# Weight loads moved to another queue, and a residual read back in quarters, in the down-projection of a hybrid decoder layer

## The chip, the cores and the metric

The kernel runs on one core of a Trainium2 chip. A core has five engines that run side by side, each through its own list of instructions in a fixed order: TensorE (PE in the profile: the matmuls, and PEld: the weight loads into its array), VectorE (DVE), ScalarE (ACT), GpSimd (POOL) and SyncE (SP). Transfers between the main memory (HBM) and the on-chip memory are issued by SP, ACT or POOL and carried out by 16 shared DMA engines; an instruction that issues a transfer first waits for what it needs, and everything behind it on that engine waits with it. The metric is device time in microseconds (us) for one launch.

## The reference, cut to what matters

One trunk layer for 512 tokens of width 1024. An attention sub-layer gives a residual stream x; then follows a gated MLP whose down-projection is the place of the change:

```python
def conv_ffn(h, w_up, conv_w, conv_b, w_down):
    u = h @ w_up                       # 1024 -> 2 * 2816
    up = jnp.pad(u, ((0, 0), (CONV_WIDTH - 1, 0), (0, 0)))
    c = conv_b + conv_w[0] * up[:, 0:s]
    for j in range(1, CONV_WIDTH):
        c = c + conv_w[j] * up[:, j:j + s]
    val, gate = jnp.split(c, 2, axis=-1)
    return (jax.nn.silu(gate) * val) @ w_down      # 2816 -> 1024
...
        h2 = rmsnorm(x, ffn_norm_g[l])
        x = x + conv_ffn(h2, w_up[l], conv_w[l], conv_b[l], w_down[l]).astype(x.dtype)
```

All values are float32.

## The kernel before, in words

Float32 products are made from pairs of a high and a low part: ACT copies a weight tile `raw` to its rounded high part `whi`, DVE subtracts to get the low part `wlo` (`wsplit_`, L288 to L306), and PE multiplies high by high, low by high and high by low. `raw` has three buffers, `whi` and `wlo` two each. `wload` (L271) issues the next load of the list `weight_tiles` from SP. A load must wait until the `wlo` of the tile three places earlier has been made, since that read the same buffer; a `whi` must wait until PE has read the one two places earlier.

The up-projection (L1385 to L1402) makes 22 blocks of 128 features. In each, the convolution is built in `cgq` by ACT and DVE, and the result is split into parts for the down-projection. Before it, the residual `x1` (2 MB) was written to main memory as `x1d` (L1354); its room is used otherwise.

The down-projection (L1475 to L1574) uses a scheme with seven products in place of eight for a two by two partition: the 2816 weight rows come in 11 pairs of 128 rows (g = 0 to 10), the tokens in two halves, the columns in two halves. One product of a pair, both token tiles of a half, is six matmuls (four with `whi`, two with `wlo`). It runs in four stretches; inside them the order on every engine is that of the code:

- **The first pass** (L1481 to L1493) uses six pieces of weights, here called A0 to A5: A0 holds one pair, the others two pairs each.
- **The second pass** (L1494 to L1508) uses six more, B0 to B5, in the same way.
- **The loop over pairs** (L1511 to L1542) makes four products per pair from sums of the four weight blocks of the pair. DVE makes these sums in place in the raw tiles: `sum_13` (two additions; the first reads only the first 128 rows of the pair, the second both), then `sum_24` (two more). `sum_hi` lets ACT copy the high parts, `sum_lo` lets DVE make the low parts.
- **The last pass** (L1545 to L1574) uses the pieces for the seventh product, while the results are added to the residual (`add_to`, in part on POOL) and stored.

The raw tiles of the odd pairs come through `wload`. Those of the even pairs go to `sraw` (two tiles of 512 KB), which lies in the room of `cgq`: `sum_load` (L1432 to L1440) issues them from SP, so for pair 0 SP waits there until the last convolution no longer needs `cgq`. `sum_load(0)` stands ahead of the whole first pass (L1478), `sum_load(2)` in its last step, the others in the loop. For pair 0, `sum_13` runs in step 3 of the first pass, `sum_24` and `sum_hi` in step 4, `sum_lo` in step 5. In step i of a pass, `produce` splits piece i+1 and loads piece i+3 of the same list.

The residual is read back into `x1b` by one POOL transfer (L1406), as soon as the room of the up-projection's input is free; its first use is `add_to(0, 0, P2)` in the second pass (L1499), the next POOL's addition at the start of the loop (L1525), the rest after the loop.

Of the kernel before, what the change touches and what calls it, by code (L numbers as in the profile page):

```python
# [21 lines left out]
NT = S // 128  # L22
# [60 lines left out]
def hybrid_block(ctx: ExitStack, tc: tile.TileContext, A: dict, out: bass.AP):  # L83
    nc = tc.nc
# [24 lines left out]
    def bank(tag, bufs, shape=(128, 512)):  # L109
        return ps.tile(list(shape), F32, name="ps_" + tag, tag=tag, bufs=bufs)  # L110

    def mmb():
        return bank("mm", 4)

    def pa():
        return bank("a", 2)
# [154 lines left out]
    def wload():  # L271
        nxt = next(wtiles, None)
        if nxt is not None:
            src, kt, n, eng = nxt
            raw = wp.tile([128, kt, n], F32, name="raw", tag="raw", bufs=3)
            nc.sync.dma_start(raw, src if len(src.shape) == 3 else src.rearrange("(k p) n -> p k n", p=128))
            loads.append((raw, kt, n, eng))
# [997 lines left out]
    x1 = xr.tile([128, NT, D], F32, name="x1", tag="x1")  # L1275
# [39 lines left out]
    with tc.manual_schedule(engines=KTS):  # L1315
        for t in range(NT):
            qs = slice(128 * t, 128 * t + 128)
            p = mmb()
# [34 lines left out]
    x1d = dp.tile([128, NT * D], F32, name="x1d")  # L1353
# [31 lines left out]
    for f in range(NF):  # L1385
# [4 lines left out]
        g = f // 2  # L1390
# [12 lines left out]


    x1 = xr.tile([128, NT, D], F32, name="x1b", tag="hh2")
    nc.gpsimd.dma_start(x1.rearrange("p t d -> p (t d)"), x1d)  # L1406
    ring = xr.tile([128, 2, 2, 2, 512], F32R, name="ring", tag="hl2")
    sraw = cgq[:, 0:8].rearrange("p (r a) n -> p r (a n)", r=2)

    def product(banks, x, w, first=False, end=False, ts_=(0, 1)):  # L1410

        for n, (x_, y) in enumerate(((x[0], w[0]), (x[1], w[0]), (x[0], w[1]))):
            for t in ts_:
                mm(banks[t], x_[:, 128 * t:128 * t + 128], y, first and n == 0, end and n == 2)

    def res(t, c, n=512, c0=0):
        return x1[:, t, 512 * c + c0:512 * c + c0 + n]

    def add_to(half, c, src, op=ALU.add, eng=None):
        for i in range(2):  # L1420
            o = res(2 * half + i, c)
            (eng or v).tensor_tensor(o, o, src[i], op=op)  # L1422

    def store(half, c):
        for t in (2 * half, 2 * half + 1):
            nc.gpsimd.dma_start(out[0][128 * t:128 * t + 128, 512 * c:512 * c + 512], res(t, c))  # L1426
# [3 lines left out]
    raws = {}  # L1430

    def sum_load(g):  # L1432
        if g >= NG:
            return
        if g % 2:
            raws[g] = [loads.pop(0)[0][:, 0] for _ in range(2)]
        else:
            raws[g] = [sraw[:, i] for i in range(2)]
            for i in range(2):
                nc.sync.dma_start(raws[g][i], A["w_down"][0][256 * g + 128 * i:256 * g + 128 * i + 128])  # L1440

    def sum_13(g):
        if g < NG:
            b1, b2 = raws[g]
            tt(b1[:, 0:512], b1[:, 0:512], b1[:, 512:1024], ALU.add)
            tt(b1[:, 512:1024], b1[:, 512:1024], b2[:, 512:1024], ALU.add)

    def sum_24(g):
        if g < NG:
            b1, b2 = raws[g]  # L1450
            tt(b2[:, 512:1024], b2[:, 512:1024], b1[:, 0:512], ALU.add)
            tt(b2[:, 0:512], b2[:, 0:512], b2[:, 512:1024], ALU.add)

    def sum_hi(g, i):
        if g % 2:
            hi = wp.tile([128, 2, 512], F32R, name="whi", tag="whi", bufs=2)
            lo = wp.tile([128, 2, 512], F32R, name="wlo", tag="wlo", bufs=2)
        else:
            hi, lo = ring[:, i, 0], ring[:, i, 1]
        act(hi, raws[g][i].rearrange("p (b n) -> p b n", b=2))  # L1460
        return hi, lo

    def sum_lo(g, i, hi, lo):
        tt(lo, raws[g][i].rearrange("p (b n) -> p b n", b=2), hi.bitcast(F32), ALU.subtract)
        return [(hi[:, b], lo[:, b]) for b in range(2)]

    def produce():
        wsplit()
        wload()
# [6 lines left out]
    with tc.manual_schedule(engines=everything):  # L1476
        wload()
        sum_load(0)  # L1478
        P2, P1 = [mmb(), mmb()], [pa(), pa()]
        T = {}  # L1480
        for i, gs in enumerate(DOWN):  # L1481
            w = ahead.pop(0)
            produce()
            if i == 3:
                sum_13(0)
            elif i == 4:
                sum_24(0)
                h = [sum_hi(0, 0), sum_hi(0, 1)]
            elif i == 5:
                T[0] = [sum_lo(0, k, *h[k]) for k in range(2)]  # L1490
                sum_load(2)
            for j, g in enumerate(gs):
                product(P2, (a2[:, 0, g, 0], a2[:, 1, g, 0]), [x[:, j] for x in w], g == 0, g == NG - 1)  # L1493
        for i, gs in enumerate(DOWN):  # L1494
            w = ahead.pop(0)
            if i < len(DOWN) - 1:
                produce()
            if i == 1:
                add_to(0, 0, P2)  # L1499
            elif i == 2:  # L1500
                two_parts(a2[:, 0, 0:6, 0], a2[:, 1, 0:6, 0], ql[:, 0:6])
            elif i == 3:
                two_parts(a2[:, 0, 6:NG, 0], a2[:, 1, 6:NG, 0], ql[:, 6:NG])
            elif i == 5:
                sum_load(1)
                sum_13(1)
            for j, g in enumerate(gs):
                product(P1, (a1[:, 0, g], a1[:, 1, g]), [x[:, j] for x in w], g == 0, g == NG - 1)  # L1508
        u = [[ql[:, 4 * k + 2 * t:4 * k + 2 * t + 2].rearrange("p a n -> p (a n)") for t in range(2)] for k in range(2)]
        P4, P5, P7 = [mmb(), mmb()], [mmb(), mmb()], [pb(), pb()]  # L1510
        for g in range(NG):  # L1511
            n, last = g + 1, g == NG - 1
            if not last:
                h13 = sum_hi(n, 0)
                sum_24(n)
                h24 = sum_hi(n, 1)
                T[n] = [sum_lo(n, 0, *h13), sum_lo(n, 1, *h24)]
                if n % 2:
                    wload()
                    wload()  # L1520
                sum_load(n + 2)
                if g == 0:
                    act_copy(u[0], P1)
                    P6 = [pa(), pa()]
                    add_to(0, 0, u[0], eng=nc.gpsimd)  # L1525
                    store(0, 0)
                if g in (2, 4, 6):
                    k = g // 2 - 1
                    two_parts(a1[:, 0, k], a1[:, 1, k], q4[k])
                if g == NG - 2:  # L1530
                    two_parts(a1[:, 0, 3:5], a1[:, 1, 3:5], ql[:, 14:16])
                    two_parts(a1[:, 0, 5:7], a1[:, 1, 5:7], cgq[:, 8:10])
                sum_13(g + 2)
            else:
                produce()
                produce()
                two_parts(a1[:, 0, 7:NG], a1[:, 1, 7:NG], cgq[:, 10:14])
            (t1, t3), (t4, t2) = T.pop(g)
            product(P5, split[D1][g], t1, g == 0, last)
            product(P7, split[D3][g], t3, g == 0, last)  # L1540
            product(P4, (a2[:, 0, g, 1], a2[:, 1, g, 1]), t4, g == 0, last)
            product(P6, split[N2][g], t2, g == 0, last)  # L1542
        add_to(1, 0, P7)
        add_to(1, 1, P7, ALU.subtract)
        P3 = [pb(), pb()]  # L1545
        for i, gs in enumerate(DOWN[:-2]):
            w = ahead.pop(0)
            for j, g in enumerate(gs):
                product(P3, split[Q4][g], [x[:, j] for x in w], g == 0)
            produce()  # L1550
            if i == 0:
                add_to(1, 0, P4)
            elif i == 1:
                for t in range(2):
                    tt(u[0][t], u[0][t], P6[t], ALU.add)
                add_to(1, 0, u[0], eng=nc.gpsimd)
                store(1, 0)
            elif i == 2:
                for t in range(2):
                    tt(u[1][t], u[0][t], P5[t], ALU.add)  # L1560
                for h_ in (1, 0):
                    add_to(h_, 1, u[1], ALU.subtract, nc.gpsimd)
                    if h_:
                        store(1, 1)
        ends = [(gs, ahead.pop(0)) for gs in DOWN[-2:]]
        for t in range(2):
            for gs, w in ends:
                for j, g in enumerate(gs):
                    product(P3, split[Q4][g], [x[:, j] for x in w], False, g == NG - 1, ts_=(t,))
            n = 256 if t else 512  # L1570
            for c0 in range(0, 512, n):
                o = res(t, 1, n, c0)
                tt(o, o, P3[t][:, c0:c0 + n], ALU.subtract)
                (sc if c0 else nc.sync).dma_start(out[0][128 * t:128 * t + 128, 512 + c0:512 + c0 + n], o)  # L1574
# [28 lines left out]
```

## Time and profile before

| | |
|---|---|
| time, median of 3 runs | 854.68 us (854.37 to 855.96) |
| the profiled execution | 856.35 us, of which 854.2 us are the span that the profile shows |
| transfers issued by SP, whole run | 80.59 MB, 32.3% of the 16 DMA engines' time |
| transfers issued by POOL, whole run | 7.62 MB, 2.7% |

The profile is of one execution, on the same clock throughout, in microseconds from the start of the span. A row of its time order gives start, length, engine, line of the code, operation and, in brackets, how long the engine had been idle and what released it. A line can be that of a helper: L122 is every matmul, L125 every ACT copy, L276 every `wload`, L305 every `wlo` of a piece, L128 the other DVE additions and subtractions, L1440 the loads of `sum_load`. The view by stretches gives, for a stretch of time, the busy time of each engine with the number of its instructions, and then the TensorE clock that was granted (1.00 is full speed) and the share of the DMA engines in use.

### The profile page before, as it was taken

The page shows a single profiled execution, that of the slowest core. Times are in us where ns is not written, and L with a number is a line of the kernel's source. Part 1 is how long each engine was busy: PE and PEld are TensorE (multiplying, and loading weights), DVE is VectorE, ACT ScalarE, POOL GpSimd, SP SyncE. Part 2 cuts the span into 40 slices and gives each one's busy share as a digit, 9 for nine tenths or more (in the row PEclk, how much of TensorE's full clock was granted, in tenths as well). Part 3 has the DMA queues.
Part 4 walks back from the last instruction along what each step waited for, and adds up shares of the span by engine and source line. Part 5 has one row for each costly group of instructions (what it writes and reads, how often), then busy time and mean ns, then how long its engine had stood idle before and what let it go on. Part 6 is the DMA issues. An engine that isn't in the chain of part 4 may idle for free.

```text
span 854.2 us, 13060 instructions
## 1 busy us (share of the span) xinstructions
PE 823.0 (96%) x5039; PEld 669.3 (78%) x5039; DVE 603.0 (71%) x1150; ACT 440.1 (52%) x845; POOL 68.9 (8%) x85
## 2 busy tenths in 40 slices
PE   7999999999999999999999999999999999689996
PEld 5877878887777886777788888888888888468885
DVE  4578779963555678888675666666667666569984
ACT  6776654552545677767343454444444444344441
POOL 5200010040000010111000000000000000002005
PEclk9999999999999999999999999999999999799999
DMA  7513222335462330010166233333333332755652
GB/s 217 133 50 79 82 75 75 77 106 165 124 123 51 79 72 13 17 35 26 51 231 201 99 98 93 93 95 93 97 99 99 98 99 62 258 194 176 196 160 99
DMA packets 110706, 91.59 MB, mean 107 GB/s; under 512 B 4189, under 2 KB 98068, under 8 KB 110388
## 3 DMA queue, kind: packets, MB, share of 16 engines
q1 hardware_dynamic: 107344, 80.59, 32.3%
q0 software_dynamic: 2240, 7.62, 2.7%
q10 hardware_dynamic: 1060, 2.55, 1.0%
q8 instruction: 39, 0.64, 0.3%
q14 instruction: 23, 0.19, 0.1%
HBM read 85.30 MB, written 4.39 MB: 105 GB/s over the span
## 4 chain that ended last, share of the span: by engine, by line
PE 48%; DMA 2%; DVE 1%; POOL 1%; ACT 0%; issue 0%; SPq 0%; POOLq 0%; DVEq 0%; ACTq 0%
PE ps_mm L122 42%; PE ps_a L122 3%; PE ps_b L122 3%; DMA raw<-in_w_down_dram 2%; POOL x1b L1422 1%; DVE hl L137 0%; DVE wlo L305 0%; ACT whi L125 0%; POOL out_dram L1426 0%; PE ps_b L1211 0%; PE ps_a L202 0%; PE ps_mm L1211 0%; DVE cgq L137 0%; DVE cgq L128 0%; ACT hh L125 0%
## 5 line engine op out<-in xcount | busy, mean ns | idle before, releaser
L122 PE MATMUL ps_mm<-hh,whi 128*128 128x512 f32 (+1 forms) x624 | 242.8, 391 | 0.4 <-ACT hh L125 0.3
L122 PE MATMUL ps_mm<-hl,whi 128*128 128x512 f32 (+1 forms) x624 | 239.0, 385 | 0.3 <-DVE hl L137 0.2
L305 DVE TENSOR_TENSOR wlo<-raw,whi 128x1024 fp32r<-128x1024 f32 (+1 forms) x107 | 125.1, 1170 | 110.2 <-PE ps_mm L122 71.4
L125 ACT ACTIVATE whi<-raw 128x1024 fp32r<-128x1024 f32 (+2 forms) x130 | 128.5, 989 | 124.4 <-PE ps_mm L122 55.9
L122 PE MATMUL ps_mm<-hh,wlo 128*128 128x512 f32 (+1 forms) x624 | 152.7, 384 | 0.0
L122 PEld LDWEIGHTS ps_mm<-hh,whi 128*128 128x128 f32 x624 | 117.2, 188 | 26.3 <-ACT hh L125 0.8
L122 PEld LDWEIGHTS ps_mm<-hl,whi 128*128 128x128 f32 x624 | 117.3, 188 | 23.3 <-DVE hl L137 1.0
L122 PEld LDWEIGHTS ps_mm<-hh,wlo 128*128 128x128 f32 x624 | 115.1, 188 | 23.3
L137 DVE SCALAR_TENSOR_TENSOR cgq<-ps_mm,cw,cgq 128x511 f32<-128x511 f32 (+1 forms) x88 | 65.4, 746 | 1.6
L125 ACT ACTIVATE cgq<-ps_mm,cw 128x512 f32<-128x512 f32 x44 | 34.4, 781 | 19.3 <-PE ps_mm L122 18.7
L125 ACT ACTIVATE P<-P,nm 128x512 f32<-128x512 f32 (+3 forms) x64 | 35.4, 553 | 14.9 <-DVE nm L1185 14.9
L125 ACT ACTIVATE a<-cgq 128x512 fp32r<-128x512 f32 (+2 forms) x24 | 13.2, 550 | 56.6 <-DVE cgq L128 56.6
L128 DVE TENSOR_TENSOR cgq<-cgq 128x512 f32<-128x512 f32 (+1 forms) x52 | 36.4, 700 | 1.7 <-ACT cgq L125 0.3
L125 ACT ACTIVATE cgq<-cgq 128x512 f32<-128x512 f32 x22 | 13.9, 633 | 45.2 <-DVE cgq L137 45.2
L1185 DVE CUSTOM_DVE_ANT_0 P<-ps_a,AB 128x512 f32<-128x512 f32 (+3 forms) x64 | 29.3, 482 | 4.2 <-PE ps_a L122 3.7
L305 POOL TENSOR_TENSOR wlo<-raw,whi 128x512 fp32r<-128x512 f32 (+3 forms) x13 | 20.4, 1570 | 136.0 <-PE ps_mm L122 57.3
L122 PE MATMUL ps_mm<-whi,a 128*128 128x512 f32 x64 | 19.0, 422 | 8.2 <-ACT whi L125 8.2
L122 PE MATMUL ps_a<-KH,qst 128*128 128x512 f32 (+3 forms) x64 | 21.3, 348 | 1.5 <-DVE nm L1185 0.9
L122 PE MATMUL ps_mm<-whi,hh 128*128 128x280 f32 (+2 forms) x72 | 22.6, 333 | 0.2 <-DVE AB L128 0.2
L125 ACT ACTIVATE QK<-ps_mm 128x64 f32<-128x64 f32 (+5 forms) x56 | 14.9, 308 | 14.4 <-PE ps_mm L122 14.3
L125 ACT ACTIVATE ring<-cgq 128x1024 fp32r<-128x1024 f32 x12 | 12.7, 1061 | 18.5 <-DVE cgq L128 14.7
L122 PEld LDWEIGHTS ps_mm<-whi,a 128*128 128x128 f32 x64 | 13.0, 205 | 11.4 <-ACT whi L125 8.6
(425 smaller groups left out, 1489.5 us busy)
## 6 DMA issues: line engine op xcount, KB each, us to landing
raw<-in_w_up_dram SPq DMA_DIRECT2D x44, 512.0 KB, 3.8
raw<-in_w_in_dram SPq DMA_DIRECT2D x38, 512.0 KB, 4.0
raw<-in_w_down_dram SPq DMA_DIRECT2D x25, 512.0 KB, 4.2
cgq<-in_w_down_dram SPq DMA_DIRECT2D x12, 512.0 KB, 3.7
raw<-in_w_out_dram SPq DMA_DIRECT2D x8, 512.0 KB, 3.6
xt<-in_x_dram SPq DMA_DIRECT2D x4, 512.0 KB, 5.8
raw<-in_cmp_w_k_dram SPq DMA_DIRECT2D x4, 512.0 KB, 3.8
raw<-in_cmp_w_v_dram SPq DMA_DIRECT2D x4, 512.0 KB, 4.5
```

What stands on the lines that cost most here:

```text
L122: te.matmul(o, lhsT=l, rhs=r, start=start, stop=stop)
L125: sc.activation(o, i, f, **kw)
L128: v.tensor_tensor(o, a, b, op=op)
L137: v.scalar_tensor_tensor(o, a, s, b, op0=op0, op1=op1)
L305: eng.tensor_tensor(lo, raw, hi.bitcast(F32), op=ALU.subtract)
L1185: v.tensor_tensor_reduce(out=P[:, i], in0=sp[:, N * (i - i0):N * (i - i0) + N], in1=BT[:, h, 384 - 128 * qt:512], scale=-1.0, scalar=-NEG, ...
L1422: (eng or v).tensor_tensor(o, o, src[i], op=op)
```

## The change

The loads of `sum_load` are issued by POOL's queue and no longer by SP's. The single read-back of the residual becomes four of 512 KB (two token tiles by 512 columns), each issued where the code now says `reload`: the first ahead of the first pass, right behind `sum_load(0)`, the others in the loop at g = 3, 5 and 7, right behind a `sum_load`.

```diff
     x1 = xr.tile([128, NT, D], F32, name="x1b", tag="hh2")
-    nc.gpsimd.dma_start(x1.rearrange("p t d -> p (t d)"), x1d)
...
+    def reload(half, c):
+        h_ = slice(2 * half, 2 * half + 2)
+        nc.gpsimd.dma_start(x1[:, h_, 512 * c:512 * c + 512],
+                            x1d.rearrange("p (t d) -> p t d", t=NT)[:, h_, 512 * c:512 * c + 512])
...
             for i in range(2):
-                nc.sync.dma_start(raws[g][i], A["w_down"][0][256 * g + 128 * i:256 * g + 128 * i + 128])
+                nc.gpsimd.dma_start(raws[g][i], A["w_down"][0][256 * g + 128 * i:256 * g + 128 * i + 128])
...
         wload()
         sum_load(0)
+        reload(0, 0)
...
                     store(0, 0)
+                if g in (3, 5, 7):
+                    reload(*((1, 0), (1, 1), (0, 1))[g // 2 - 1])
```

On SP, from the first load of the down-projection on, the order before is this (128x512 is a piece of one pair, 128x2x512 of two, `cgq` the loads of an even pair, 128x1024 those of an odd one):

```order
L276 DMA raw<-in_w_down_dram 128x512
L276 DMA raw<-in_w_down_dram 128x2x512 x2
L1440 DMA cgq<-in_w_down_dram 128x1024 x2
L276 DMA raw<-in_w_down_dram 128x2x512 x3
L276 DMA raw<-in_w_down_dram 128x512
L276 DMA raw<-in_w_down_dram 128x2x512 x2
L1440 DMA cgq<-in_w_down_dram 128x1024 x2
L276 DMA raw<-in_w_down_dram 128x2x512 x3
```

With the change the same stretch of SP's list, and a little beyond, is this:

```order
L276 DMA raw<-in_w_down_dram 128x512
L276 DMA raw<-in_w_down_dram 128x2x512 x5
L276 DMA raw<-in_w_down_dram 128x512
L276 DMA raw<-in_w_down_dram 128x2x512 x5
L276 DMA raw<-in_w_down_dram 128x1024 x10
```

So A3 to A5 stand directly behind A0 to A2, and B3 to B5 directly behind B0 to B2, with nothing of the even pairs between them. Those loads are now on POOL, whose list with the change reads so, from the start of the down-projection to the first addition after the loop (L1444 is the load of `sum_load`, L1425 a `reload`, L1421 POOL's `add_to`, L1430 a store):

```order
L1444 DMA cgq<-in_w_down_dram 128x1024 x2
L1425 DMA x1b<-x1d 128x2x512
L1444 DMA cgq<-in_w_down_dram 128x1024 x2
L1421 TENSOR_TENSOR x1b<-x1b,ql 128x512 x2
L1430 DMA out_dram<-x1b 128x512 x2
L1444 DMA cgq<-in_w_down_dram 128x1024 x4
L1425 DMA x1b<-x1d 128x2x512
L1444 DMA cgq<-in_w_down_dram 128x1024 x2
L1425 DMA x1b<-x1d 128x2x512
L1444 DMA cgq<-in_w_down_dram 128x1024 x2
L1425 DMA x1b<-x1d 128x2x512
L1421 TENSOR_TENSOR x1b<-x1b,ql 128x512 x2
```

Before, POOL had only the one read-back ahead of the first two additions here; now two loads and a quarter stand ahead of the next two loads, and the three other quarters lie between the loads of the loop. The last convolution belongs to a part whose order a scheduler chooses, and there DVE's list moves too, at the seam between the up-projection and the first pass (- before, + with the change; `a_5128` and `d_5129` are parts of the activations, `cgq<-ql,cgq` is the last use of the convolution's room, the `cgq` row with x2 is `sum_13` of pair 0):

```order
 L128 TENSOR_TENSOR cgq<-cgq 128x512
 L128 TENSOR_TENSOR cgq<-cgq 128x256
-L137 SCALAR_TENSOR_TENSOR ql<-cgq 128x256
+L305 TENSOR_TENSOR wlo<-raw,whi 128x1024
 L128 TENSOR_TENSOR a_5128<-cgq,a_5128 128x512
 L128 TENSOR_TENSOR d_5129<-cgq,d_5129 128x256
+L137 SCALAR_TENSOR_TENSOR ql<-cgq 128x256
 L137 SCALAR_TENSOR_TENSOR cgq<-ql,cgq 128x256
-L305 TENSOR_TENSOR wlo<-raw,whi 128x1024 x2
+L305 TENSOR_TENSOR wlo<-raw,whi 128x1024
 L128 TENSOR_TENSOR cgq<-cgq 128x512 x2
 L305 TENSOR_TENSOR wlo<-raw,whi 128x1024
```

The `wlo` of A3 has moved ahead of the last four small operations of the convolution, and with it the last use of `cgq` is one `wlo` later. On ACT the `whi` of A3 moves ahead of two copies in the same way. PE's order is unchanged.

## The prediction

> **What bounds the kernel now.** I read the head of the page first, then the chain of work that ended last, then the stretches in which PE stands still, then the queue that PE waits for.
>
> ```profile
> span 854.2 us, 13060 instructions
> PE 823.0 (96%) x5039; PEld 669.3 (78%) x5039; DVE 603.0 (71%) x1150; ACT 440.1 (52%) x845; POOL 68.9 (8%) x85
> ```
>
> PE is the bound on the average, but an average says nothing of the down-projection. The chain, in order of time from 700 us on, does:
>
> ```profile
> 732.94 6.50 DMA raw<-in_w_down_dram
> ...
> 740.65 10.72 PE ps_mm L122 x36
> ...
> 754.07 6.53 DMA raw<-in_w_down_dram
> ...
> 761.82 10.17 PE ps_a L122 x36
> ...
> 838.65 3.55 POOL x1b L1422 x2
> ```
>
> Twice the chain leaves PE for a weight load of 6.5 us. What that costs is in the view by stretches (start:end, length, busy time and number per engine, granted clock, DMA share, GB/s), asked for PE's gaps, the stretches behind them, and the loop over pairs:
>
> ```profile
> 732.30:740.65 8.35, 0.17 (x1) 0.00 (x0) 0.20 (x2) 1.06 (x1) 0.00 (x0) 0.68 0.88 325
> 740.65:745.76 5.11, 5.11 (x12) 4.00 (x13) 3.72 (x4) 1.50 (x2) 0.00 (x0) 0.52 0.45 134
> 753.48:754.77 1.29, 0.16 (x2) 0.01 (x1) 1.29 (x3) 0.00 (x0) 0.00 (x0) 1.00 0.84 216
> 759.43:761.82 2.39, 0.17 (x2) 0.01 (x1) 0.03 (x1) 1.11 (x2) 0.00 (x0) 1.00 0.98 375
> 761.82:766.36 4.54, 4.54 (x13) 3.30 (x13) 4.39 (x4) 3.74 (x4) 0.00 (x0) 0.62 0.37 133
> 771.82:831.66 59.84, 59.84 (x265) 49.55 (x264) 57.05 (x68) 25.64 (x29) 4.59 (x4) 1.00 0.56 180
> ```
>
> The loop gives PE's undisturbed price: 44 products in 59.84 us, 1.36 us each. The two passes hold 22 products, 29.9 us, but run from 725.50 to 771.82:
>
> ```profile
> 725.50 1.07 PE L122 MATMUL ps_mm<-whi,a 128*128 128x512 f32 x4
> ...
> 771.82 1.52 PE L122 MATMUL ps_mm<-ring,d 128*128 128x512 f32 x6
> ```
>
> That is 46.3 us, so 16.4 us are lost: 8.35 idle; 5.11 - 2.72 = 2.39 because the next two products ran at a clock of 0.52; 1.29 idle; 2.39 idle; 4.54 - 2.72 = 1.82 at 0.62; 0.2 of rest. No more than 16.4 us can be won here.
>
> The cause is SP's queue:
>
> ```profile
> SPq L1440 <- DVE cgq L128: 13.7, 1, 13.7
> 730.25 0.35 SPq L1440 DMA_DIRECT2D cgq<-in_w_down_dram  x1
> 732.94 1.54 SPq L276 DMA_DIRECT2D raw<-in_w_down_dram  x3
> 720.26 0.69 DVE L305 TENSOR_TENSOR wlo<-raw,whi 128x512 fp32r<-128x512 f32 x1 [0.25 <-PE ps_mm L122]
> ```
>
> A0's `wlo` ends at 720.95, so A3's buffer is free then; but SP stands for 13.7 us at the load of pair 0, and A3 goes out at 732.94. It then shares the DMA engines (0.88 in use) with two loads of pair 0 and the 2 MB residual. B3 is held the same way by pair 2.
>
> **The change part by part.** Step 1, **A3 to A5 early.** With the loads of pair 0 gone from SP, A3 is issued at 721.0.
>
> ```profile
> raw<-in_w_down_dram SPq DMA_DIRECT2D x25, 512.0 KB, 4.2
> cgq<-in_w_down_dram SPq DMA_DIRECT2D x12, 512.0 KB, 3.7
> 725.76 1.23 DVE L305 TENSOR_TENSOR wlo<-raw,whi 128x1024 fp32r<-128x1024 f32 x1 [3.14 <-PE ps_mm L122]
> 728.22 1.07 PE L122 MATMUL ps_mm<-whi,a 128*128 128x512 f32 x4
> 728.35 1.21 DVE L305 TENSOR_TENSOR wlo<-raw,whi 128x1024 fp32r<-128x1024 f32 x1
> 730.65 0.43 DVE L137 SCALAR_TENSOR_TENSOR ql<-cgq 128x256 f32<-128x256 f32 x1
> 732.05 0.43 DVE L137 SCALAR_TENSOR_TENSOR cgq<-ql,cgq 128x256 f32<-128x256 f32 x1
> ```
>
> At 4.2 us it lands near 725. ACT makes its `whi` when PE has read A1's (728.22 + 1.07 = 729.3), to 730.4; DVE reaches its `wlo` at 730.65, in the place where the `ql` row stood, and ends at 731.8. PE wants A3 at 732.30: no wait, 8.35 + 2.39 = 10.7 us saved. A4 and A5 follow A1's and A2's `wlo` (725.76 + 1.23 = 727.0, 728.35 + 1.21 = 729.6) and land by 734; PE wants them at 735.0 and 737.7.
>
> Step 2, **what is late next: the second load of pair 0.** It waits for the last use of `cgq`, which ended at 732.48. One `wlo` (1.14 us from start to start) now stands ahead of it, so it ends at 733.6 and POOL issues at 733.7. A 512 KB load on POOL's queue is nowhere in this trace; its neighbours on that queue are
>
> ```profile
> out_dram<-x1b POOLq DMA_DIRECT2D x6, 256.0 KB, 2.5
> x1b<-x1d POOLq DMA_DIRECT2D x1, 2048.0 KB, 7.7
> ```
>
> so between 2.5 and 7.7 us. A straight line between them gives 3.2, the same load on SP's queue takes 3.7; I take 3.7, landing at 737.4. The second addition of `sum_13` waits for it, and behind that on DVE and ACT stand, in this order, A5's `wlo`, `sum_24`, the second `sum_hi` and B0's `whi`. Before, they ran:
>
> ```profile
> 746.41 1.23 DVE L305 TENSOR_TENSOR wlo<-raw,whi 128x1024 fp32r<-128x1024 f32 x1 [1.93 <-ACT whi L125]
> 747.56 1.41 DVE L128 TENSOR_TENSOR cgq<-cgq 128x512 f32<-128x512 f32 x2
> 749.00 1.06 ACT L125 ACTIVATE ring<-cgq 128x1024 fp32r<-128x1024 f32 x1 [1.67 <-DVE cgq L128]
> 749.97 0.61 ACT L125 ACTIVATE whi<-raw 128x512 fp32r<-128x512 f32 x1
> ```
>
> From the `wlo`'s start to the end of `whi` 4.17 us; with half of `sum_13` (0.7) PE can start B0 4.9 us after the landing, at 742.3. PE would be ready after A3 to A5, 732.3 + 3 x 2.72 = 740.46. So a wait of **1.85 us**, partly within A5 (its `wlo` ends at 739.3, PE wants it at 738.6).
>
> Step 3, **B1.** DVE makes both `sum_lo` of pair 0 ahead of B1's `wlo`, so PE waited 1.29 us there already. From the end of B0's `whi` (750.58) to PE going on (754.77) are 4.19 us, all DVE work; a product's four `whi` matmuls are 0.91 of its 1.36 us, so PE had begun B0 at 753.48 - 0.91 - 1.36 = 751.21, 0.63 us after its `whi`; now it begins at once and waits 1.29 + 0.63 = **1.92 us** and goes on at 742.3 + 4.2 = 746.5.
>
> Step 4, **B3.** Its buffer is free with B0's `wlo`, at 743.0; it lands near 747.2, and PE wants it at 746.5 + 0.45 + 1.36 + 2.72 = 751.0. The 2.39 + 1.82 us go. B4 and B5 come earlier than that still. The first quarter is issued behind the second load, near 734.3; its 7.7 us at most end ahead of `add_to`, at 747 or later. From B1 on PE has 0.45 us and 9 products, 12.7 us: the loop begins at **759.2**, not 771.82.
>
> Step 5, **the loop.** DVE has almost no air in it:
>
> ```profile
> 780.25 1.59 SPq L1440 DMA_DIRECT2D cgq<-in_w_down_dram  x2
> 781.41 2.86 DVE L128 TENSOR_TENSOR raw<-raw 128x512 f32<-128x512 f32 x4
> 787.01 2.86 DVE L128 TENSOR_TENSOR cgq<-cgq 128x512 f32<-128x512 f32 x4
> 792.28 2.87 DVE L128 TENSOR_TENSOR raw<-raw 128x512 f32<-128x512 f32 x4
> 822.09 2.57 DVE L128 TENSOR_TENSOR ring<-cgq,ring 128x1024 fp32r<-128x1024 f32 x2
> 826.22 1.52 PE L122 MATMUL ps_mm<-ring,d 128*128 128x512 f32 x6
> ```
>
> Two pairs take DVE 10.87 us (781.41 to 792.28), PE 8 x 1.36 = 10.88. The second load of pair 4 goes out when `sum_lo` ends, 781.5, and is wanted by the second addition at 787.7: a window of 6.2 us. At 3.7 it fits; at 7.7 it is 1.5 late, four times, while DVE's lead at the end is 3.8 us (the first half of the 822.09 row ends at 823.3, its low part is wanted 0.91 after 826.22). I cost it at nothing. POOL is idle there but for its two additions and two stores early in the loop, so nothing holds its queue; the other quarters land long before the loop ends.
>
> On POOL an issue takes 0.55 us, with DVE busy beside it:
>
> ```profile
> 777.03 1.11 POOL L1426 DMA_DIRECT2D out_dram<-x1b  x2
> ```
>
> The Trainium skill speaks against the change: "SBUF — State Buffer", section "SBUF: two separate sides", says that transfers issued from GpSimd are starved while DVE runs in a two-port mode, and "A bandwidth-pool intuition that's wrong" puts 620 ns against 3100 ns; by that (an estimate from the page) each load would take 2.5 us more and the sum would be 844.6. "Who interferes with whom" there exempts `tensor_tensor`, and the row above agrees: DVE was in one.
>
> The last pass and the tail after it (771.82 to the end) hang on PE and on POOL's additions as before. **Sum:** lost before 16.4 us, lost after 1.85 + 1.92 = 3.8, gain 12.6 us. The profiled execution took 856.35 us, 854.2 of span and 2.15 around it; 856.35 - 12.6 = 843.7. It stands 1.67 above the median of the runs, 854.68, so I forecast 854.68 - 12.6 = **842.1 us**.
>
> **The rivals.** *The clock falls again.* A gap of 2.39 us was followed by 0.62, one of 1.29 was not. Mine are 1.85 (in two pieces) and 1.92, between them. One fall costs 1.82 to 2.39: 844.2. For: they lie close together. Against: each is under 2.39. The Trainium skill, "TensorE: Matmul & The Clock Gate", section "What's actually happening", wants an idle window of about 3.4 us; by it neither gap would slow the clock. The trace differs: 2.39 us sufficed.
>
> *POOL's loads are slow.* At 7.7 us the wait of step 2 grows by 4.0, the loop loses 4 x 1.5 - 3.8 = 2.2: 848.3; with only the first, 846.1. For: more packets share the engines. Against: 7.7 was for four times the bytes.
>
> *Slower.* The same lateness, in the loop alone: every microsecond past the window of 6.2 is paid at four loads, since DVE never catches up, and once in step 2. With x for the landing the gain is 12.6 - (x - 3.7) - (4(x - 6.2) - 3.8) = 44.9 - 5x; from 9.3 us on the kernel is slower by more than 0.2%, at 10 us it takes 859.8. Against: no POOL transfer took over 7.7.
>
> *The change does nothing,* because A3 is held by something other than the load ahead of it: 854.7. Against: SP's 13.7 us names the cause.
>
> *Better than the sum:* the second load lands in 2.5 us and DVE's operations close up; at most all 16.4, 838.3.
>
> **How the numbers follow.** The sum as it stands (840.9 to 843.2, landings of 2.5 to 4.8 us) 0.50; the clock falls 0.18; POOL slow 0.14; better 0.08; nothing 0.04; slower 0.06. A measurement can tell about 0.2% (1.7 us). Faster 0.50 + 0.18 + 0.14 + 0.08 = 0.90, same 0.04, slower 0.06. The range of 840.0 to 847.5 leaves out the last two cases, half of "better" and a third of "POOL slow", 0.19.
>
> **What would show it.** Right: SP issues A3 near 721; PE has no gap ahead of A3 and B3; gaps of about 1.9 us at B0 and B1; the loop starts near 759 at 59.8 us long; the loads on POOL land in 3 to 5 us. Wrong: a clock under 0.9 between 738 and 760 (first rival), a landing over 6 us or DVE waiting for `cgq` in the loop (second and third), A3's issue still behind 730 (fourth).

## The result, and the profile after

The changed kernel took 846.47 us (median of 4 runs, 845.63 to 848.40) against 854.52 us beside it: a ratio of 0.9909, 95% interval 0.9885 to 0.9933. It is faster, by 8.1 us where 12.6 were forecast. The profiled execution took 845.63 us.

The head of the page of the changed kernel: PE's busy time is 2.8 us less than before, though it does the same matmuls; the two stretches at a lowered clock are gone from the passes.

```profile
span 843.8 us, 13072 instructions
...
PE 820.2 (97%) x5039; PEld 667.2 (79%) x5039; DVE 602.9 (71%) x1150; ACT 439.6 (52%) x845; POOL 77.6 (9%) x100
```

In the time order of PE and of SP, the first matmuls of the first pass and of the loop, and SP's loads from A3 on:

```profile
725.30 1.07 PE L122 MATMUL ps_mm<-whi,a 128*128 128x512 f32 x4
...
760.16 1.52 PE L122 MATMUL ps_mm<-ring,d 128*128 128x512 f32 x6
```

```profile
720.81 14.01 SPq L276 DMA_DIRECT2D raw<-in_w_down_dram  x5
```

The two passes take 34.86 us in place of 46.32. A3 goes out at 720.81, at once after A0's `wlo`, and no longer at 732.94. The view by stretches of PE's gaps (at A5, B0 and B1), of what is behind the last of them, and of the loop (columns as before: start:end, length, busy time and number per engine, granted clock, DMA share, GB/s):

```profile
738.61:740.07 1.46, 0.00 (x1) 0.00 (x1) 1.46 (x3) 1.06 (x1) 0.00 (x0) 1.00 0.70 282
...
742.17:743.00 0.83, 0.00 (x1) 0.00 (x0) 0.01 (x1) 0.83 (x3) 0.00 (x0) 1.00 0.96 373
745.57:747.14 1.57, 0.00 (x1) 0.00 (x1) 1.57 (x3) 0.00 (x0) 0.87 (x2) 1.00 1.02 292
747.14:760.16 13.02, 13.02 (x56) 10.54 (x57) 10.83 (x11) 5.97 (x6) 0.00 (x0) 1.00 0.75 255
760.16:820.55 60.39, 60.01 (x266) 49.40 (x264) 57.71 (x70) 26.22 (x30) 11.00 (x15) 1.00 0.63 207
```

No gap stands ahead of A3 or B3, and the clock is 1.00 in all these stretches. Three gaps of 3.86 us in all are left, where the idle time alone was 12.0 before. The loop is 0.55 us longer than before. What the gaps hang on is in the time order of POOL and of DVE (the two loads of pair 0, the first quarter; then the additions of `sum_13`, the `wlo` of A5, `sum_24` and the `wlo` of B0):

```profile
730.56 0.54 POOL L1444 DMA_DIRECT2D cgq<-in_w_down_dram  x1 [246.72 <-DVE cgq L128]
733.86 0.53 POOL L1444 DMA_DIRECT2D cgq<-in_w_down_dram  x1 [2.76 <-DVE cgq L137]
734.38 0.73 POOL L1425 DMA_DIRECT2D x1b<-x1d  x1
```

```profile
736.07 0.69 DVE L128 TENSOR_TENSOR cgq<-cgq 128x512 f32<-128x512 f32 x1 [1.64 <-DMA cgq<-in_w_down_dram]
738.19 0.69 DVE L128 TENSOR_TENSOR cgq<-cgq 128x512 f32<-128x512 f32 x1 [1.43 <-DMA cgq<-in_w_down_dram]
738.80 1.22 DVE L305 TENSOR_TENSOR wlo<-raw,whi 128x1024 fp32r<-128x1024 f32 x1
739.93 1.41 DVE L128 TENSOR_TENSOR cgq<-cgq 128x512 f32<-128x512 f32 x2
742.99 0.69 DVE L305 TENSOR_TENSOR wlo<-raw,whi 128x512 fp32r<-128x512 f32 x1 [1.64 <-ACT whi L125]
```

The second load is issued at 733.86, and DVE, idle for 1.43 us, goes on with it at 738.19: 4.3 us. A5's `wlo` stands behind that addition, so PE waits for the even pair's load through a piece that has nothing to do with it.

### The profile page after: what moved, and what is told of

The parts are those of the page before. It is cut to its first block, busy times and chain, and to the rows that moved or that the text cites. A ratio compares the mean times of both kernels' runs of the same rounds, so it can differ in the third digit from the quotient of the medians.

```text
span 843.8 us, 13072 instructions
## 1 busy us (share of the span) xinstructions
PE 820.2 (97%) x5039; PEld 667.2 (79%) x5039; DVE 602.9 (71%) x1150; ACT 439.6 (52%) x845; POOL 77.6 (9%) x100
## 5 line engine op out<-in xcount | busy, mean ns | idle before, releaser
L1444 POOL DMA_DIRECT2D cgq<-in_w_down_dram x12 | 6.4, 535 | 291.4 <-DVE cgq L128 246.7
L125 ACT ACTIVATE ring<-cgq 128x1024 fp32r<-128x1024 f32 x12 | 12.7, 1062 | 22.1 <-DVE cgq L128 16.7
L122 PE MATMUL ps_mm<-whi,hl 128*128 128x280 f32 (+2 forms) x72 | 21.7, 323 | 0.0
```

The source lines that it names most:

```text
L122: te.matmul(o, lhsT=l, rhs=r, start=start, stop=stop)
L125: sc.activation(o, i, f, **kw)
L1444: nc.gpsimd.dma_start(raws[g][i], A["w_down"][0][256 * g + 128 * i:256 * g + 128 * i + 128])
```

## The experiments

All ratios are to the kernel before, measured beside each (854.4 to 854.9 us); they are taken over all runs, so they can differ a little from the ratio of the medians. "Landing" is the time from the start of the issue of pair 0's second load to the addition of DVE that waited for it; "passes" and "loop" are read from the time order of PE, as above, in one profiled execution each. "Sums" are `sum_13`, `sum_24`, `sum_hi` and `sum_lo`.

| kernel | median us (range) | ratio, 95% interval | passes | loop | landing |
|---|---|---|---|---|---|
| the change, first set | 846.47 (845.63 to 848.40) | 0.9909 [0.9885, 0.9933] | 34.86 | 60.39 | 4.3 |
| e0_change | 848.58 (847.48 to 848.63) | 0.9919 [0.9906, 0.9933] | 38.13 | 60.41 | 6.3 |
| e10_change_again | 849.59 (846.57 to 849.60) | 0.9935 [0.9920, 0.9949] | 39.27 | 59.93 | 7.4 |
| e1_queue_only | 847.17 (846.57 to 848.27) | 0.9907 [0.9894, 0.9921] | 36.77 | 59.92 | 5.6 |
| e2_quarters_only | 854.84 (853.36 to 855.48) | 0.9994 [0.9985, 1.0003] | 45.58 | 59.91 | |
| e3_order_on_sp | 846.38 (844.25 to 847.02) | 0.9888 [0.9873, 0.9903] | 33.47 | 62.16 | 3.7 |
| e5_quarters_on_sp | 843.84 (843.03 to 845.39) | 0.9875 [0.9860, 0.9889] | 33.48 | 61.51 | 3.7 |
| e11_quarter_beside_sp | 843.56 (842.81 to 844.58) | 0.9872 [0.9853, 0.9890] | 33.39 | 61.63 | 3.6 |
| e7_quarter_first | 845.97 (844.70 to 848.09) | 0.9900 [0.9884, 0.9916] | 34.27 | 59.84 | 3.9 |
| e4_sums_later | 845.73 (845.10 to 846.12) | 0.9894 [0.9879, 0.9909] | 33.97 | 61.00 | no wait |
| e9_hi_behind_b3_pool | 846.04 (844.52 to 846.61) | 0.9898 [0.9884, 0.9911] | 34.13 | 61.80 | 7.2 |
| e6_sums_later_sp | 843.56 (843.14 to 843.93) | 0.9869 [0.9852, 0.9885] | 31.99 | 61.79 | no wait |
| e8_hi_behind_b3 | 842.32 (841.86 to 842.75) | 0.9859 [0.9844, 0.9874] | 31.02 | 61.81 | no wait |

**Which part of the change does it.** Two kernels take one part each. `e1_queue_only` has the loads on POOL's queue and the residual in one piece (the edits below are against the change):

```diff
+    nc.gpsimd.dma_start(x1.rearrange("p t d -> p (t d)"), x1d)
...
-        reload(0, 0)
...
-                if g in (3, 5, 7):
-                    reload(*((1, 0), (1, 1), (0, 1))[g // 2 - 1])
```

> Only the queue: the loads of the even pairs on POOL's queue, the residual still read back in one piece of 2 MB at the old place. Theory (what counts is that A3 and B3 no longer stand behind loads that wait): no gap ahead of A3 or B3; but the 2 MB go out near 726, ahead of the loads of pair 0 on the same queue, so the second of them lands 1 to 3 us later than with quarters and B0 starts as much later: gain 7 to 9.5 us, 845 to 848. Rival (the 2 MB burst was what made A3 late): a gap of some us stays ahead of A3 or A4, gain under 4 us.

`e2_quarters_only` has the quarters and leaves the loads on SP:

```diff
-                nc.gpsimd.dma_start(raws[g][i], A["w_down"][0][256 * g + 128 * i:256 * g + 128 * i + 128])
+                nc.sync.dma_start(raws[g][i], A["w_down"][0][256 * g + 128 * i:256 * g + 128 * i + 128])
```

> Only the quarters: the residual in four pieces as with the change, the loads of the even pairs on SP's queue as before. Theory: A3 still goes out behind the load of pair 0 near 732.9, but lands in 4 to 5 us in place of 6.5, so the first gap shrinks from 8.35 to about 6 us, the clock falls as before, the second gap stays: gain 1.5 to 3 us, 852 to 853. Rival (the burst was the cause): gain 6 us or more.

The queue alone gives 7.8 us, inside its theory and no less than the change, which gained 6.4 beside it (`e0_change`); the quarters alone give 0.1, which their interval does not tell from nothing. That second expectation was missed. The stretches of `e2_quarters_only` say where its gain went: the gap ahead of A3 and the two products behind it, then the same at B3.

```profile
732.32:738.48 6.16, 0.00 (x0) 0.00 (x1) 0.03 (x2) 1.06 (x1) 0.00 (x0) 0.72 0.89 328
738.48:743.59 5.11, 5.11 (x16) 4.09 (x17) 3.72 (x4) 2.03 (x3) 0.00 (x0) 0.67 0.55 187
756.92:759.89 2.97, 0.00 (x1) 0.01 (x1) 0.02 (x1) 1.11 (x2) 0.00 (x0) 0.84 0.82 310
759.89:764.43 4.54, 4.54 (x11) 3.57 (x12) 4.39 (x4) 3.42 (x3) 0.00 (x0) 0.50 0.35 124
```

Without the 2 MB beside it A3 arrives 2.2 us sooner (8.35 us of gap become 6.16). But 0.6 of that is lost in the gap at B3, and the clock behind it is 0.50 in place of 0.62, with 11 matmuls in the stretch in place of 13. In all the passes are 0.7 us shorter, in one profile. What holds A3 is SP's standing, and that is as long as before; the traffic beside it is the smaller part. In `e1_queue_only` the 2 MB cost a gap of 0.96 us ahead of A4, and its loop is undisturbed:

```profile
762.37:822.29 59.92, 59.92 (x266) 49.40 (x264) 57.74 (x70) 26.39 (x30) 8.86 (x12) 1.00 0.55 182
```

**Is it POOL's queue, or the order on SP's?** `e3_order_on_sp` leaves the loads on SP and issues those of pair 0 behind A5, those of pair 2 behind B5. Nothing then stands behind a load that waits for long:

```diff
-                nc.gpsimd.dma_start(raws[g][i], ...
+                nc.sync.dma_start(raws[g][i], ...
...
-        sum_load(0)
...
-            if i == 3:
+            if i == 2:
+                sum_load(0)
+            elif i == 3:
                 sum_13(0)
...
-                sum_load(2)
...
+                sum_load(2)
```

> The loads of the even pairs on SP's queue as before, but those of pair 0 issued behind A5 and those of pair 2 behind B5; the residual in quarters on POOL as with the change. Theory (it is the order of the waits, not the queue): no gap ahead of A3 and B3, the loads of pair 0 land in about 3.7 to 5 us, and no load of the loop is late, so the time is that of the change or up to 1.5 us better: 843.5 to 846. Rival (a queue of their own is needed): gaps ahead of A3 or B3 come back, or B0's load, now behind the second load of pair 0, holds B0; 848 or more.

The order on SP does as much as a queue of its own, 846.38 us, 0.4 over the theory's range, and its passes, 33.47 us, are shorter than the change's. It loses part of that in the loop, where POOL's three quarters are no longer held apart by loads that wait. In its time order of POOL and its stretch behind that:

```profile
767.02 2.14 POOL L1425 DMA_DIRECT2D x1b<-x1d  x3
```

```profile
766.96:776.00 9.04, 9.04 (x41) 7.48 (x41) 8.72 (x11) 4.21 (x5) 2.20 (x4) 1.00 0.94 325
```

All three go out at once, the DMA engines are 0.94 in use, DVE waits for loads, and the last pass begins 2.05 us late (time order of PE). Behind that gap the clock is 0.52 and 0.50 from 822.5 to 824 and from 824 to 826:

```profile
821.02 1.47 PE L122 MATMUL ps_b<-whi,a 128*128 128x512 f32 x4 [2.05 <-DVE x1b L1421]
```

`e5_quarters_on_sp` puts these three quarters on SP, behind the loads of their step (against `e3_order_on_sp`):

```diff
-                    reload(*((1, 0), (1, 1), (0, 1))[g // 2 - 1])
+                    reload(*((1, 0), (1, 1), (0, 1))[g // 2 - 1], eng=nc.sync)
```

> As the kernel with all loads on SP behind A5 and B5, but the three later quarters issued on SP behind the loads at g = 3, 5, 7 and not in one burst on POOL behind the two stores. Theory (that burst made the load of pair 4 land in 7.6 us, DVE lost 2 us of its lead and PE waited 2.05 us at the last pass): DVE does not wait in pair 4, the gap ahead of the last pass is under 0.6 us, 844 to 845.5. Rival (DVE's lead was lost by something else, as the order of SP's loads in the loop): the gap stays at 1.5 us or more, 846 or later.

The gap ahead of the last pass falls from 2.05 to 0.86 us, not under 0.6 as expected, and the time by 2.5 us; the clock behind the gap stays at 1.00. POOL issues no load then but the first quarter, and the slowest of this kernel's runs, 845.39, is under the fastest of the change's 13, 845.63.

**Why the change itself comes out so differently.** It was run twice more, `e0_change` beside the first experiments and `e10_change_again` beside the last.

> The change itself, timed again against the kernel before, since the four runs of it (845.63 to 848.4) leave the gain between 5.7 and 9.8 us while the two profiled executions lie 10.7 apart. Theory (the sum of the traces): the gain is the 11.5 us by which the loop starts earlier in the profiled run, less 0.6 at the loop's end and some tenths behind it: 844 to 845, gain 9.5 to 10.5. Rival (some executions lose TensorE clock behind the gaps at B0 and B1, 2 us each time): median 846 to 847, gain about 8, with a spread of 2 us or more between its runs.

> The change once more, for a third profile of it. Theory: the time of the passes goes with the landing of the second load of pair 0. At 4.3 us after its issue they took 34.9 us, at 6.2 us 38.1 with a slower clock behind a gap of 3.4 us. So: landed in under 4.5 us, passes of 34 to 35 us and the clock at 1.00; landed in over 5.5 us, 37 us or more, and a clock under 0.95 just behind the gap at A5. Median 846 to 848.6. Rival: the passes take 37 us or more with an early landing, or under 35.5 with a late one.

`e0_change` came out over both numbers expected of it. `e10_change_again` bears out the theory in landing, passes and clock, and its median lies 1.0 us over the range given. In `e0_change` the second load and the addition that waits for it (time order of POOL, of DVE), and the gap at A5 with what is behind it (stretches):

```profile
733.33 0.53 POOL L1444 DMA_DIRECT2D cgq<-in_w_down_dram  x1 [2.76 <-DVE cgq L137]
```

```profile
739.60 0.69 DVE L128 TENSOR_TENSOR cgq<-cgq 128x512 f32<-128x512 f32 x1 [2.99 <-DMA cgq<-in_w_down_dram]
```

```profile
738.08:741.48 3.40, 0.00 (x1) 0.01 (x1) 1.88 (x3) 1.06 (x1) 0.00 (x0) 1.00 0.35 143
741.48:746.00 4.52, 4.52 (x12) 3.15 (x13) 2.85 (x4) 2.52 (x3) 0.00 (x0) 0.62 0.38 116
```

And in `e10_change_again`:

```profile
733.59 0.53 POOL L1444 DMA_DIRECT2D cgq<-in_w_down_dram  x1 [2.76 <-DVE cgq L137]
```

```profile
740.98 0.69 DVE L128 TENSOR_TENSOR cgq<-cgq 128x512 f32<-128x512 f32 x1 [3.62 <-DMA cgq<-in_w_down_dram]
```

```profile
738.34:742.87 4.53, 0.01 (x1) 0.01 (x1) 1.89 (x3) 1.06 (x1) 0.00 (x0) 0.81 0.33 131
742.87:748.10 5.23, 5.23 (x13) 4.12 (x14) 3.56 (x5) 2.63 (x3) 0.00 (x0) 0.51 0.39 107
```

The landing is 4.3, 6.3 and 7.4 us in the three profiles, and the gap at A5 follows it: 1.46, 3.40 and 4.53. Behind the last two the clock falls (0.62, 0.51), which adds some 2 us. So in these three profiles the passes go with one number, the landing of one load.

What makes that load late, the quarter that is issued right behind it or the queue? `e7_quarter_first` issues the quarter ahead of the loads of pair 0, so it has gone before them:

```diff
         wload()
-        sum_load(0)
         reload(0, 0)
+        sum_load(0)
```

> The change, with the first quarter of the residual issued ahead of the loads of pair 0 on POOL and not behind them. In the two profiled executions of the change the second load of pair 0 took 4.3 and 6.2 us to land, while on SP's queue it took 3.6. Theory (the quarter and the loads of A5 and B0 share the DMA engines with it, so its landing varies): with the quarter gone by 731 it lands in 3.6 to 4.5 us, DVE waits under 1.5 us for it, and the time is 845 to 847, 1 to 2 us under the change. Rival (POOL's queue is slow by itself): it lands in 5 to 6.5 us as before, 847.5 to 849.

```profile
733.81 0.54 POOL L1444 DMA_DIRECT2D cgq<-in_w_down_dram  x1 [2.75 <-DVE cgq L137]
```

```profile
737.72 0.69 DVE L128 TENSOR_TENSOR cgq<-cgq 128x512 f32<-128x512 f32 x1 [1.24 <-DMA cgq<-in_w_down_dram]
```

The theory holds in landing (3.9 us), wait (1.24) and median (845.97), but the profiled run was the fastest of four that still spread from 844.70 to 848.09. The other half of the question is `e11_quarter_beside_sp`: as `e5_quarters_on_sp`, with the first quarter on SP too, right behind the loads of pair 0.

```diff
-        reload(0, 0)
...
             if i == 2:
                 sum_load(0)
+                reload(0, 0, eng=nc.sync)
```

> The version with the loads and the loop's quarters on SP (843.84 us, second load of pair 0 landed 3.3 us after its issue, passes 33.48 us), with the first quarter issued by SP too, right behind the two loads of pair 0, so that it moves beside the second of them as in the change. It tells what makes that load land in 4.3 to 7.4 us in the change. Theory: sharing the DMA engines with the quarter does it, whatever the queue: the second load lands in 4.2 us or more, the passes take 34.3 us or more, and the time is 844.6 to 848. Rival: it is POOL's queue: it lands in under 3.9 us, the passes stay under 34, and the time is 843.3 to 844.6.

The rival's numbers came (the 3.3 us that it starts from count from the end of the issue, 3.7 from its start). SP's loads and the quarter, and DVE's addition:

```profile
730.21 3.67 SPq L1444 DMA_DIRECT2D cgq<-in_w_down_dram  x2
734.18 0.38 SPq L1425 DMA_DIRECT2D x1b<-x1d  x1
```

```profile
737.08 0.69 DVE L128 TENSOR_TENSOR cgq<-cgq 128x512 f32<-128x512 f32 x1 [1.88 <-DMA cgq<-in_w_down_dram]
```

The second issue begins near 733.5 (730.21 + 3.67 less the 0.37 of one issue) and lands in 3.6 us with the quarter right behind it, and the four runs lie within 1.8 us. On SP's queue the same load lands in 3.6 to 3.7 us in all three profiles that show it, on POOL's in 3.9 to 7.4 in six. But the company of the load changes with its queue: SP issues B0's and B1's loads only behind it, while in the first profile of the change B0's, issued at 731.58, is under way, and B1's follows 0.6 us behind. So the quarter alone does not make the load late; that POOL's queue alone does is not shown.

**Taking the wait away.** `e4_sums_later` is the change with pair 0's sums one stretch later, so that A5, B0 and B1 don't stand behind them:

```diff
-            if i == 3:
+            if i == 5:
                 sum_13(0)
-            elif i == 4:
-                sum_24(0)
-                h = [sum_hi(0, 0), sum_hi(0, 1)]
-            elif i == 5:
-                T[0] = [sum_lo(0, k, *h[k]) for k in range(2)]
-                sum_load(2)
...
                 add_to(0, 0, P2)
+                sum_24(0)
+                h = [sum_hi(0, 0), sum_hi(0, 1)]
...
+            elif i == 4:
+                T[0] = [sum_lo(0, k, *h[k]) for k in range(2)]
+                sum_load(2)
```

> The change, with the sums of pair 0 moved later: sum_13 into step 5 of the first pass, sum_24 and sum_hi into step 1 of the second, sum_lo and the loads of pair 2 into step 4. Theory (what is left of the loss is the wait for the second load of pair 0, with DVE's sums behind it): the gaps at A5, B0 and B1 go, and the clock stays up; in the second look at the change the passes took 38.1 us, here 30 to 32.5, so 841.5 to 844.5 and some 5 us better than the change. Rival (DVE is the bound of the second pass, which now holds 5 us more of its work): gaps open at B3 to B5 or ahead of the loop, passes of 34 us or more, 845 or later.

The three gaps go, and one of 2.24 us opens at B3, with a product at half the clock behind it: ACT's second `sum_hi` waits for `sum_24` in front of B3's `whi`. The time is 1.2 us over the theory's range, in the rival's.

```profile
747.40:749.64 2.24, 0.00 (x0) 0.00 (x1) 0.17 (x2) 2.05 (x3) 0.00 (x0) 0.96 0.30 114
749.64:752.36 2.72, 2.72 (x6) 2.15 (x7) 2.57 (x2) 2.72 (x3) 0.00 (x0) 0.50 0.20 18
```

`e6_sums_later_sp` makes the same edit in `e5_quarters_on_sp`.

> Both at once: all loads on SP with the quarters between them, and the sums of pair 0 later. Theory: passes of 30 to 32 us and no gap over 0.6 us ahead of the last pass: 841 to 843.5, the fastest of all. Rival (DVE bound): as above, 844 or later.

There the gap at B3 is 1.06 us, and the clock stays up. The passes are 31.99 us, as the theory has it, but the 1.5 us won there against `e5_quarters_on_sp` don't show in the medians, 843.56 and 843.84, whose ranges overlap; the gap ahead of the last pass is 0.84 us, not under 0.6. `e8_hi_behind_b3` moves the two `sum_hi` one step later, behind B3's `whi`; `e9_hi_behind_b3_pool` does so in `e4_sums_later`:

```diff
                 sum_24(0)
-                h = [sum_hi(0, 0), sum_hi(0, 1)]
             elif i == 2:
+                h = [sum_hi(0, 0), sum_hi(0, 1)]
```

> The version with the loads and the loop's quarters on SP and pair 0's sums later (843.56 us), with one more step: ACT's two sum_hi of pair 0 stand behind the whi of B3, not ahead of it. Theory: its 1.06 us gap ahead of B3 came only from the second sum_hi waiting for sum_24 in front of that whi; it goes, the passes take about 31 us in place of 31.99, and the time is 842.3 to 843.2. Rival: the sum_hi now hold the whi of B4 or B5 in the same way, the gap moves there with its 1 us, and the time stays at 843.3 to 844.

> The change with pair 0's sums later (845.73 us) and ACT's two sum_hi behind the whi of B3. There the gap ahead of B3 was 2.24 us, and matmuls behind it ran at under full clock. Theory: both go, the passes take 31 to 31.8 us in place of 33.97, and the time is 842.8 to 844 (the loop still pays the quarters, some 0.5 to 1 us). Rival: the second load of pair 0 on POOL's queue lands so late that sum_24 is late for B4 as well: a gap of 1 to 2 us there, 844.5 to 846.

`e8_hi_behind_b3` met its theory in time and passes and is the fastest kernel of the study, 842.32 us, 12.1 under the kernel before beside it; its slowest run, 842.75, is just under the fastest of all others, 842.81. Its stretch over both passes:

```profile
724.85:755.87 31.02, 30.25 (x133) 24.62 (x132) 25.66 (x29) 16.11 (x17) 0.74 (x1) 1.00 0.64 212
```

PE stands for 0.77 us in them, at B4, one of the places that the rival named. Its loop is long, 61.81 us: PE comes to it earlier than DVE can follow, and waits at its end for DVE's additions to the residual.

```profile
817.68 1.47 PE L122 MATMUL ps_b<-whi,a 128*128 128x512 f32 x4 [0.84 <-DVE x1b L1421]
```

`e9_hi_behind_b3_pool` gains nothing, and not for the reason that its rival gave. No gap is left at B3 and one of 0.61 us stands at B4, where the rival expected 1 to 2, but a longer one opens at B1. ACT's row of that place, and the stretches:

```profile
743.15 2.20 ACT L125 ACTIVATE whi<-raw 128x1024 fp32r<-128x1024 f32 x2 [5.42 <-DMA raw<-in_w_down_dram]
```

```profile
741.60:744.26 2.66, 0.00 (x0) 0.00 (x1) 0.02 (x1) 1.06 (x1) 0.00 (x0) 1.00 0.53 203
744.26:747.01 2.75, 2.69 (x10) 1.91 (x11) 2.75 (x3) 1.06 (x1) 0.00 (x0) 1.00 0.19 42
```

Here it is SP's own load, B1's, that lands late, beside the load and the quarter on POOL's queue. So with two queues at work the lateness can strike either.

**What is late in a late load.** The trace records the landing of a load in 16 parts. In `e0_change`, 14 parts of pair 0's second load are in 3.7 us after its issue, the last two after 6.1 and 6.2; in `e10_change_again` 13 are in after 3.8, the last three after 6.8 to 7.3; in `e9_hi_behind_b3_pool` 12 after 3.8, the last four after 6.7 to 7.1; in the first profile of the change all are in after 4.2. Only in `e1_queue_only` are all 16 late alike, after 4.8 to 5.5. B1's load, which SP issues 0.6 us later, lags in the same way: 14 parts after 4.5 us and two after 7.7 and 7.8 in `e0_change`, 13 after 4.6 and three after 8.3 to 8.9 in `e10_change_again`. In the five kernels that load pair 0 on SP's queue behind A5, the last part of the second load is in after 3.4 to 3.6 us. So most of the load is nearly as early on POOL's queue as long as the residual comes in quarters; a few parts lag, in the loads of both queues. And POOL's queue is not slow by itself: in the loop, where hardly anything moves beside it, the first load of each pair lands in 3.7 to 3.9 us on that queue, 12 times out of 12 in the three profiles of the change.

One rival no run separates. The rounds ran on different chips: the record names 8 for `e0_change` to `e3_order_on_sp`, 10 for `e4_sums_later` to `e7_quarter_first`, 13 for `e8_hi_behind_b3` to `e10_change_again`, 14 for `e11_quarter_beside_sp`, and none for the first set. To the last part, the second load took 6.2 and 5.5 us on POOL's queue on chip 8, 4.8 and 3.8 on 10, 7.1 and 7.3 on 13; on SP's queue 3.4 to 3.6 on all four. So the queue and its company count on each chip on which both were run, but how late the load is may go with the chip, and no run of the change is on record for chip 14.

## Why the prediction was right in sign and too high in size

- **What bounds the kernel.** Right. SP's standing at the load of pair 0, and of pair 2, made the gaps at A3 and B3. `e1_queue_only`, `e2_quarters_only` and `e3_order_on_sp` show it from three sides: taking the even pairs' loads out of the way of A3 and B3 brings 7.8 us by another queue and 8.6 by the order, and the quarters alone bring nothing that can be measured. "The change does nothing" falls with that.
- **Step 1** (A3 to A5 early) and **step 4** (the gap at B3 goes) held: A3's issue at 720.81 (forecast 721.0), no gap there, the clock at 1.00.
- **Step 2** named what is late next and mis-sized it: this is the step that failed. It gave the second load of pair 0 the 3.7 us that such a load takes on SP's queue. Measured were 4.3, 6.3 and 7.4 us in three profiles of the change: 0.6, 2.6 and 3.7 more, and in the last two some 2 us of lowered clock behind the gap, which the sum left out. The rest of the step's chain was right: 4.9 us from the landing to B0 were forecast, 743.00 - 738.19 = 4.8 measured. The bounds of 2.5 to 7.7 us held all the values; the choice inside them was wrong. POOL's queue does land such a load in 3.7 to 3.9 us when hardly anything moves beside it, as the loop shows; the step left out the company, B0's and B1's loads on SP's queue and the quarter. Which of these makes parts of the load late is not shown.
- **Step 3.** 1.92 us forecast at B1, 1.57 measured.
- **Step 5** costed the loop at nothing. It took 0.55 us more in the first profile and in `e0_change`, of which 0.4 is a gap ahead of the last pass behind a late load of pair 10; in `e10_change_again`, where PE came later, and in `e1_queue_only`, without quarters, it took 0.1 more.
- **The sum, for the profiled executions.** 843.7 us were forecast against the profile of before, 845.63 came. The 1.9 between them: passes 34.86 for 33.7, 1.2 late, of which the landing is 0.6, the earlier start of the passes and the later issue of the load 0.4, and the stretch from B1 to the loop, 13.02 for 12.7, 0.3; the loop 0.55; the time from the last pass to the span's end 23.25 for 22.54, 0.7 late, which was forecast as unchanged; less 0.5 at the beginning and outside the span.
- **The median.** The first set's median lies 4.4 us over the forecast: those 1.9; 0.84, since the profiled execution was the fastest of its set; and the 1.67 by which the profile of before stood over its own median. I took the losses of that execution off the median as if they were the same in every run. Whether the median run loses less in the passes can't be told from one profile of before.
- **The range.** 840.0 to 847.5 us held the first set's median, 846.47, but not those of the two later sets, 848.58 and 849.59. That the first set came inside is in part luck: its profile has the shortest of the three landings.
- **The rivals.** "The clock falls again" and "POOL's loads are slow" are one case, not two: a late landing makes the gap, and the gap makes the fall. `e0_change` and `e10_change_again` show both together, and cost more (848.6, 849.6 us) than the highest that either was priced at alone, 848.3. I gave them 0.32 as separate cases, and no chance to both at once. "Slower" needed landings of 9.3 us in the loop; the longest there, in the three profiles, was 6.0 us.

What stays open: why a few parts of the loads fall behind, and why on one occasion and not on another. They do so by up to 4.3 us where loads of both queues move together (B1's load in `e10_change_again`), and by some 2 us where SP's move alone (`e3_order_on_sp`, the load issued at 747.14: eight parts in after 4.0 us, the last after 6.2). No run separates the second queue, the loads that move beside, and the chip.

## What to carry to other kernels

Where a page shows an issuing engine standing at one load with others queued behind it, move the waiting load behind the others before giving it to another queue: here the order gave 8.6 us, and with the later quarters on the same queue and the sums moved as well 12.1. A load that is to move beside the loads of another queue needs a price with them beside it, and slack for its spread; with a chain behind it that has none, its lateness is paid in full, and again in the clock: between the first and the third profile of the change 3.1 us of landing cost 4.4 us of the passes. After a wait is removed, look at which instruction now stands ahead of the next piece on each engine: A5, then B3, then the loop's end took their turn here.

## What the runs showed of the hardware

- A transfer of 512 KB issued by POOL landed in 3.9 to 7.4 us at one place of the program, counted to the addition that waited for it, by SP in 3.6 to 3.7, once with the same quarter right behind it. In the late ones most of the 16 recorded parts were in after 3.7 to 3.8 us (14 in `e0_change`, 13 in `e10_change_again`) and the rest up to 3.5 us later.
- The length of a gap alone does not tell whether the clock falls behind it: after 2.24 us (`e4_sums_later`) it was 0.50, after 2.97 (`e2_quarters_only`) 0.50, after 2.05 (`e3_order_on_sp`) 0.52 from 1.5 us behind it on, after 2.66 us (`e9_hi_behind_b3_pool`) 1.00, after 3.40 and 4.53 us 0.62 and 0.51, and after the change's 1.46 and 1.57 us 1.00. The Trainium skill, "TensorE: Matmul & The Clock Gate", section "What's actually happening", wants an idle window of about 3.4 us; the gaps of 1.46 and 1.57, 2.66, 3.40 and 4.53 us agree with it, those of 2.05, 2.24 and 2.97 us do not, nor does the one of 2.39 before the change.
- The 12 loads that POOL issued in the change took 0.53 to 0.55 us each to issue, the same as its stores took before; what grew was the time from the issue to the landing. The 3100 ns that the Trainium skill, "SBUF — State Buffer", section "A bandwidth-pool intuition that's wrong", gives for a transfer from GpSimd beside a DVE `tensor_copy`, weighed in the prediction, are of another case: between the issue and the landing of pair 0's second load DVE ran `TENSOR_TENSOR` rows alone and stood idle for the rest, 1.64 and 1.43 us in the first profile, 2.52 and 3.62 in `e10_change_again`.
